# One diffusion-transformer layer on one core: stores moved to ScalarE's queue, results of the output products added one group later

## The chip, the core and the metric

The kernel runs on one NeuronCore of a Trainium2 chip. The metric is the device time of one execution in microseconds. The core has a matrix engine (TensorE, "PE" in the profile; "PEld" is its loading of weights), a vector engine (VectorE, DVE), a scalar or activation engine (ScalarE, ACT), a general engine (GpSimd, POOL) and a synchronization engine (SyncE, SP). Each works off its own list of instructions in order; between engines they wait on semaphores. A DMA transfer is issued by an instruction in some engine's list, and runs afterwards on the DMA engines.

## The reference

The layer has 1024 latent tokens and 256 context tokens of width 1024, all in fp32. Cut to what matters:

```python
def swiglu(h, w_in, w_out):
    a, b = jnp.split(h @ w_in, 2, axis=-1)
    return (jax.nn.silu(a) * b) @ w_out

mod_lat = jax.nn.silu(c) @ w_mod + b_mod            # nine vectors ml[0..8]; mc[...] from c_ctx
x  = x  + 0.5 * ml[2] * swiglu(modulate(rms_norm(x,  g1), ml[0], ml[1]), ffn1_w_in, ffn1_w_out)
cx = cx + 0.5 * mc[2] * swiglu(modulate(rms_norm(cx, g1), mc[0], mc[1]), ffn1_w_in, ffn1_w_out)
hx = modulate(rms_norm(x, g2), ml[3], ml[4])        # the same for the context
bg, cg, vc, q, k, v, gates = split(hx @ w_in)
y_conv = bg * short_conv(cg * vc, conv_w)
o = attention(q, k, v)                              # 8 query heads, 2 key heads, QK norm, 2-D rotary
x = x + ml[5] * merge_branches(y_conv, o, gates, w_bc, w_ba, w_out)
x = x + 0.5 * ml[8] * swiglu(modulate(rms_norm(x, g3), ml[6], ml[7]), ffn2_w_in, ffn2_w_out)
return rms_norm(x, final_g)
```

The hidden width of both feed-forward blocks is 2816, 22 blocks of 128.

## The kernel before

**Precision.** Each fp32 operand is split into a high part (a cast, on ScalarE) and a low part (source minus high part, on VectorE). A product is three matmuls: high·high, high·low and low·high.

**The big products** go through the class `Winograd`, a scheme that computes a 2×2 block product with seven block products. For each pair `j` of weight columns, `first` computes products 1 and 2 (result `u`, `c`), `second` products 6, 7 and 4 (result `v`, `b`), and `third` products 5 and 3 (results `u`, `v`). One block product is twelve matmuls of 128×512. Its left operand comes from a weight load (`raw`, three buffers, loaded from SyncE's queue) or from a sum of two halves of one (`s1`, `s2`, `s3`, built on GpSimd), and is split into a tile `wl` or `wh` (four buffers each); `prefetch(4)` keeps four such tiles ready. Its right operand, `r1` to `r7`, is made once from the normalized tokens. `r1` and `r2` come from the first half of the tokens (`norm0`), `r5` and `r6` from both halves, and the "late" ones `r7`, `r4`, `r3` at the end of `norm1`.

Since products 1 and 2 need only the first half, `start` runs them for the first nine pairs (`AH2`, `AH3`) of the mixer's and of the second feed-forward block's product, while `norm1` is worked off step by step between them. All but the first two results `uc` are stored in DRAM (`put_aside`, tile `ucd`) and fetched again (`fetch`). What remains of `norm1` after that is kept as `self.late` and run in `second`. `norm1` is a generator with nine yields: the first for the row scales, the second for their broadcast, four for the columns, three for the late operands.

**The output products** of the two feed-forward blocks go through `row_products`. It takes the seven products in the order 2, 1, 4, 6, 5, 7, 3; each runs over groups of two blocks of the hidden rows, and has four banks of PSUM. Products 1, 6 and 7 add up in the same four banks (`chain`). After a product, its banks are added, with the gate as a factor, into the token tiles `x` (a table `to` says which), and a callback `after` starts what depends on it. `sums`, the additions on the hidden rows, are issued in a block in which `strict[0]` is true.

**The order of the work.** The program is handed to `TileContext(schedule_with_timeline_sim=True)`, which moves instructions within their engine's list. While `strict[0]` is true, each instruction issued through the wrapper `Engine` (its `issue` is line 88, so that nearly every row of the profile says L88) is pinned: it keeps its place in program order relative to other pinned ones.

**Modulation.** `later_mod` is a generator that computes one half of one of the nine vectors: eight loads of `w_mod` rows (`rawm`), each with a multiply-add into `macc` on VectorE and a yield; then `WAIT` yields; the split of the sum (`acch` on ScalarE, `accl` on VectorE); six yields; then two matmuls, a copy, four small DMAs and an add. It is worked off in portions: `run(steps, n)` in the loop over `j` of the first feed-forward block, `run(late_steps, n)` in the mixer (5 + 4 + 4 per `i`) and in the second feed-forward block (3 per `j`).

**Stores.** Results that go to DRAM on the way are stored by `put_aside` (`ucd`, 22 stores), `spill` (the hidden rows, `hd`, 88), `gate` (`gcd`, `gad`) and the mixer's loop (`yd`), 48 together. All of these are issued by SyncE, whose queue also issues the loads of weights, of `rawm` and of the fetched tiles.

Of the kernel before, what the change touches and what calls it, by code (L numbers as in the profile page):

```python
# [41 lines left out]
STEPS = (0, 4, 4, 4, 5, 5, 5, 5, 5, 5, 5, 2, 12)  # L42
WAIT = 4
AH1, HALVES, WH = 12, 8, (4, 5, 6, 7, 12, 13, 14, 15, 20, 21, 22, 23)
# [5 lines left out]
def tile_dit_layer(  # L50
# [211 lines left out]
    def later_mod(m, halves=(0, 1), streams=None):  # L262
# [3 lines left out]
        for half in halves:  # L266
# [15 lines left out]
            for acc in accs:  # L282
                ah, al = ttile("acch", dt=F32R), ttile("accl", dt=F32R)
                split(acc, ah, al)
                parts.append((ah, al))
            for _ in range(6):
                yield
# [178 lines left out]
    class Winograd:  # L466
# [194 lines left out]
        def start(self, norm):  # L661

            for i in range(self.n_ahead):
                t = wpool.tile([P, 2, 512], F32, tag="wh", name=uniq("uc"), bufs=W_BUFS)
                u, c = t[:, 0], t[:, 1]
                act.copy(out=u, in_=self.product(1))
                run(norm, 2 if i == 0 else 1)
                dve.tensor_add(out=c, in0=u, in1=self.product(2))
                if i < RESIDENT:
                    self.started.append((u, c))  # L670
                else:
                    self.put_aside(t)
            run(norm, 9 - self.n_ahead)
            self.prefetch(4)
            self.late = norm

        def put_aside(self, t):
            ucd = dram.tile([P, 2, 512], F32, name=uniq("ucd"))
            sp.dma_start(out=ucd[:], in_=t[:])
            self.started.append(ucd)  # L680
# [62 lines left out]
        def second(self, u):  # L743

            v, b = ttile("v"), ttile("b")
            dve.tensor_add(out=u, in0=u, in1=self.product(6))
            run(self.late, 4)
            dve.tensor_add(out=v, in0=u, in1=self.product(7))
            if self.side:
                self.side(0, self.left())  # L750
            dve.tensor_sub(out=b, in0=v, in1=self.product(4))
            run(self.late)
            return v, b

        def third(self, u, v):
# [39 lines left out]
    def row_products(w, rows, add, after=lambda i, k: None, halves=False):  # L795
# [112 lines left out]
        }  # L908
        chain = None
        for i in (2, 1, 4, 6, 5, 7) + (() if halves else (3,)):  # L910
# [3 lines left out]
            for g, (k, m) in enumerate(groups):  # L914
# [4 lines left out]
                strict[0] = True  # L919
                sums(i, g)  # L920
                strict[0] = False
                after(i, k)
            for o, ch in to[i]:
                for d in range(4):
                    add(o + d, ch, ps[d])
            after(i, rows.n)
        if halves:
            kept = []
            ps = [ps_s(256) for _ in range(4)]
            for k, m in groups:  # L930
                for lr in operands(3, k, m):
                    step(3, ps, len(kept), *lr, n=256)
                    kept.append(lr)
                after(8, k)
            for d in range(4):
# [243 lines left out]
    def spill(a, b, j, ch):  # L1179
        act.activation(out=a, in_=a, func=AF.Silu)  # L1180
        dve.tensor_mul(out=a, in0=a, in1=b)
        sp.dma_start(out=hd[j, :, ch[1] : ch[1] + 512], in_=a)

# [46 lines left out]
    for j in range(NH):  # L1230
        half1.side = side(j) if j >= SIDE_FROM else None
        if j > SIDE_FROM and j % 2:
            raws = context_rows(j)
        u, c = half1.next_first()
        v, b = half1.second(u)
        spill(c, b, j, C0)
        spill(*half1.third(u, v), j, C1)
        run(steps, STEPS[min(j, len(STEPS) - 1)])
        if j == SIDE_FROM - 1:
# [55 lines left out]
    def after1(i, k):  # L1295
# [16 lines left out]
        if k == NH // 2:  # L1312
# [4 lines left out]
            elif i == 3:  # L1317
                done(range(4), C1)
        if i == 3 and k in (0, 4):
            run(norms2, 1)  # L1320
# [19 lines left out]
    def gate(dst, j, ch, g):  # L1340
        act.activation(out=g, in_=g, func=AF.Sigmoid)
        sp.dma_start(out=dst[j, :, ch[1] : ch[1] + 512], in_=g)

    for i in range(KD):
# [6 lines left out]
        for ch, bg, gc in mixed():  # L1351
# [12 lines left out]
            dve.tensor_mul(out=y, in0=y, in1=bg)  # L1364
            sp.dma_start(out=yd[i, :, o : o + 512], in_=y)
        if i % 2:
# [475 lines left out]
    for j in range(NH):  # L1842
        if j > 1:
            run(late_steps, 3)
        u, c = fast.next_first()
        v, b = fast.second(u)
        spill(c, b, j, C0)
        spill(*fast.third(u, v), j, C1)
    run(late_steps)
    gate3 = half_gate("gate3", 8)  # L1850
# [75 lines left out]
```

## Time and profile before

| | |
|---|---|
| median of 3 runs | 2688.97 us (2684.92 to 2689.53) |
| the profiled execution itself | 2688.7 us |
| its span on the core | 2686.9 us |
| granted clock, mean | 0.993 |
| matmul instructions | 13593 |

The span goes from the first to the last instruction of the profiled execution; the rest of its time lies around that. A row of a timeline has the start in us, the duration, the engine, the line, the operation with its tiles (out<-in), and the number of such operations in a row; in brackets stands how long the engine stood idle before it, and whose work ended that. A row of waits has the waiting engine and tile, the engine and tile waited for, the total in us, the number of times and the longest. A group has its line, engine, operation and number, the busy time, the mean in ns, and the idle time before. SPq is SyncE's queue; a row of it is the issue of a DMA, not its transfer. Tile names in the profile and in the order are without their buffer numbers.

Along the span, the first feed-forward block's first product takes the time up to about 640 us, its output product up to 887, the mixer's product follows up to about 1300, then attention and merge, and the second feed-forward block ends the span.

### The profile page before, as it was taken

To read this page: it belongs to the slowest core of one execution; us is meant where nothing else is said; L and a number is where in the kernel's file an instruction comes from. 1 tells how busy PE (TensorE), PEld (TensorE's weight loads), DVE (VectorE), ACT (ScalarE), POOL (GpSimd) and SP (SyncE) were. 2 spreads that over 40 slices of the span, in tenths; PEclk is the share of its full clock that TensorE was granted. 3 is DMA by queue.
4 is the path that set the end of the run, shared out by engine and by line. 5 is a ranking of instruction groups with operands and counts; after the bars stand their busy time and mean duration, and the time that the engine had idled before them with its cause. 6 is when DMAs were issued, how large, how long until landed. Compare 5 with 4: busy or idle time off the path is not lost.

```text
span 2686.9 us, 37399 instructions
## 1 busy us (share of the span) xinstructions
PE 2643.4 (98%) x13593; PEld 2236.0 (83%) x13593; DVE 2007.1 (75%) x3356; ACT 1166.1 (43%) x2317; POOL 521.3 (19%) x409
## 2 busy tenths in 40 slices
PE   8999999999999999999999999999999999999998
PEld 5788898888788877888999888877888888888888
DVE  5888888786887889877488666775458875667875
ACT  6633543333454632333244666674236333334543
POOL 1244012121110044232033111000001533230200
PEclk9999999999999999999999999999999999999998
DMA  7655653346973445433213211002524543228731
GB/s 267 236 180 166 223 184 124 109 130 240 293 169 102 149 137 165 134 114 116 97 48 103 95 62 49 24 25 78 167 85 146 184 145 99 83 90 305 165 83 63
DMA packets 369920, 364.84 MB, mean 136 GB/s; under 512 B 27830, under 2 KB 261448, under 8 KB 369736
## 3 DMA queue, kind: packets, MB, share of 16 engines
q1 hardware_dynamic: 360712, 345.17, 39.0%
q0 software_dynamic: 9024, 17.30, 4.0%
q8 instruction: 106, 1.74, 0.3%
q14 instruction: 78, 0.64, 0.1%
HBM read 296.30 MB, written 66.06 MB: 135 GB/s over the span
## 4 chain that ended last, share of the span: by engine, by line
PE 88%; DVE 6%; DMA 2%; ACT 2%; issue 1%; SPq 1%; POOL 0%; DVEq 0%; ACTq 0%; POOLq 0%
PE ps L88 73%; PE po L88 7%; PE pt L88 7%; DMA rawm<-in_w_mod_dram 1%; DVE macc L88 1%; DVE wl L88 1%; SPq L88 1%; DVE xb L88 0%; DVE r L88 0%; ACT r L88 0%; DMA raw<-in_ffn_w_in_dram 0%; DMA xtok<-in_ctx_dram 0%; DVE ol L88 0%; DVE x L88 0%; DVE pts L88 0%
## 5 line engine op out<-in xcount | busy, mean ns | idle before, releaser
L88 PE MATMUL ps<-r,wl 128*128 128x512 f32 x5232 | 1213.4, 392 | 11.6 <-ACT wl L88 6.8
L88 PEld LDWEIGHTS ps<-r,wl 128*128 128x128 f32 x5232 | 983.9, 189 | 220.0 <-ACT wl L88 9.0
L88 ACT CAST wl<-s 128x512 fp32r<-128x512 f32 x256 | 158.0, 620 | 338.3 <-PE ps L88 266.6
L88 POOL TENSOR_TENSOR s<-raw 128x512 f32<-128x512 f32 x64 | 92.4, 1444 | 993.8 <-PE ps L88 346.6
L88 ACT CAST wl<-raw 128x512 fp32r<-128x512 f32 x286 | 176.4, 619 | 250.0 <-PE ps L88 160.6
L88 DVE TENSOR_TENSOR wl<-raw,wl 128x512 fp32r<-128x512 f32 x284 | 202.6, 717 | 68.3 <-ACT wl L88 64.7
L88 DVE TENSOR_TENSOR wl<-s,wl 128x512 fp32r<-128x512 f32 x256 | 231.8, 906 | 12.3 <-ACT wl L88 10.7
L88 POOL TENSOR_TENSOR s<-raw,s 128x512 f32<-128x512 f32 x64 | 99.8, 1560 | 363.9 <-DVE wl L88 354.4
L88 DVE SCALAR_TENSOR_TENSOR macc<-rawm,silu_c,macc 128x512 f32<-128x512 f32 x168 | 137.9, 837 | 9.5 <-DMA rawm<-in_w_mod_dram 9.1
L88 PE MATMUL ps<-wh,r 128*128 128x256 f32 x768 | 141.6, 285 | 0.0
L88 DVE TENSOR_TENSOR pts<-pt,pts 128x512 fp32r<-128x512 f32 x160 | 108.8, 687 | 39.4 <-ACT pts L88 38.4
L88 DVE TENSOR_TENSOR u<-u,ps 128x512 f32<-128x512 f32 x168 | 114.2, 680 | 28.5 <-PE ps L88 28.4
L88 DVE TENSOR_REDUCE m<-ps 128x1 f32<-128x512 f32 (+1 forms) x192 | 110.9, 596 | 31.0 <-PE ps L88 30.3
L88 ACT CAST pts<-pt 128x512 fp32r<-128x512 f32 x160 | 93.2, 593 | 88.7 <-PE pt L88 86.8
L88 ACT CAST rh<-hid 128x512 fp32r<-128x512 f32 x132 | 81.6, 621 | 112.2 <-PE ps L88 96.2
L88 PE MATMUL ps<-rh,wl 128*128 128x512 f32 x360 | 122.0, 389 | 0.0
L88 PEld LDWEIGHTS ps<-wh,r 128*128 128x128 f32 x768 | 120.6, 192 | 0.0
L88 ACT CAST wh<-raw 128x512 fp32r<-128x512 f32 (+1 forms) x88 | 69.3, 795 | 103.0 <-PE ps L88 79.5
L88 PE MATMUL po<-pts,vh 128*128 128x512 f32 x256 | 110.5, 437 | 1.5 <-ACT pts L88 1.5
L88 DVE TENSOR_TENSOR rl<-hid,rh 128x512 fp32r<-128x512 f32 x132 | 90.1, 686 | 26.5 <-ACT rh L88 13.5
L88 PE MATMUL ps<-wl,r 128*128 128x256 f32 x384 | 108.8, 283 | 0.0
L88 PE MATMUL ps<-kl,qs 128*128 128x512 f32 x384 | 105.3, 397 | 0.0
(298 smaller groups left out, 5068.1 us busy)
## 6 DMA issues: line engine op xcount, KB each, us to landing
raw<-in_ffn_w_in_dram SPq DMA_DIRECT2D x125, 512.0 KB
raw<-in_ffn_w_out_dram SPq DMA_DIRECT2D x72, 512.0 KB
rawm<-in_w_mod_dram SPq DMA_DIRECT2D x128, 256.0 KB
raw<-in_w_in_dram SPq DMA_DIRECT2D x61, 512.0 KB
hid<-hd SPq DMA_DIRECT2D x40, 512.0 KB
ws<-in_ffn_w_out_dram POOLq DMA_DIRECT2D x30, 512.0 KB, 6.6
ucd<-uc SPq DMA_DIRECT2D x22, 512.0 KB
hd<-c SPq DMA_DIRECT2D x38, 256.0 KB
```

Of the source, the lines that this page charges most:

```text
L88: inst = getattr(self.engine, name)(*args, **kw)
```

## The change

Seven edits:

1. `WAIT` goes from 4 to 2, and the second wait in `later_mod` from six yields to three.
2. In `start`, the step of `norm` is run only for `i < 9`.
3. The stores `ucd`, `hd`, `gcd`, `gad` and `yd` are issued by ScalarE (`act.dma_start`) and not by SyncE.
4. In `second`, the runs of `self.late` go through `late_operands`, which pins what they issue.
5. In `row_products`, a product's results are not added right behind it but kept in `results`, and added behind the first group of the next product, in the pinned block of `sums`; `after(i, rows.n)` moves with them. Only the last product's adds stay at its end.
6. The portions of `steps` and `late_steps` in the two feed-forward blocks are split in three and run between `next_first`, `second` and `third`, not once per `j`.
7. During product 3 of the first output product, the two steps of `norms2` run at `k` 2 and 6 and not 0 and 4.

```diff
-WAIT = 4
+WAIT = 2
...
-            for _ in range(6):
+            for _ in range(3):
                 yield
...
-                run(norm, 2 if i == 0 else 1)
+                run(norm, 2 if i == 0 else 1 if i < 9 else 0)
...
-            sp.dma_start(out=ucd[:], in_=t[:])
+            act.dma_start(out=ucd[:], in_=t[:])
...
-            run(self.late, 4)
+            self.late_operands(4)
...
-            run(self.late)
+            self.late_operands()
             return v, b
+
+        def late_operands(self, n=None):
+            strict[0] = True
+            run(self.late, n)
+            strict[0] = False
...
-        chain = None
+        chain, results = None, []
+
+        def add_results():
+            while results:
+                i, ps = results.pop()
+                for o, ch in to[i]:
+                    for d in range(4):
+                        add(o + d, ch, ps[d])
+                after(i, rows.n)
+
...
                 strict[0] = True
                 sums(i, g)
+                add_results()
                 strict[0] = False
                 after(i, k)
-            for o, ch in to[i]:
-                for d in range(4):
-                    add(o + d, ch, ps[d])
-            after(i, rows.n)
+            results.append((i, ps))
+        if not halves:
+            add_results()
...
-        sp.dma_start(out=hd[j, :, ch[1] : ch[1] + 512], in_=a)
+        act.dma_start(out=hd[j, :, ch[1] : ch[1] + 512], in_=a)
...
+        n_steps = STEPS[min(j, len(STEPS) - 1)]
         u, c = half1.next_first()
+        run(steps, n_steps // 3)
         v, b = half1.second(u)
         spill(c, b, j, C0)
+        run(steps, n_steps // 3)
         spill(*half1.third(u, v), j, C1)
-        run(steps, STEPS[min(j, len(STEPS) - 1)])
+        run(steps, n_steps - n_steps // 3 * 2)
...
-        if i == 3 and k in (0, 4):
+        if i == 3 and k in (2, 6):
             run(norms2, 1)
...
-        sp.dma_start(out=dst[j, :, ch[1] : ch[1] + 512], in_=g)
+        act.dma_start(out=dst[j, :, ch[1] : ch[1] + 512], in_=g)
...
-            sp.dma_start(out=yd[i, :, o : o + 512], in_=y)
+            act.dma_start(out=yd[i, :, o : o + 512], in_=y)
...
-        if j > 1:
-            run(late_steps, 3)
+        n_steps = j > 1
         u, c = fast.next_first()
+        run(late_steps, n_steps)
         v, b = fast.second(u)
         spill(c, b, j, C0)
+        run(late_steps, n_steps)
         spill(*fast.third(u, v), j, C1)
+        run(late_steps, n_steps)
```

What this makes of the order is shown at three places. The first is SyncE's list before, towards the end of the first block's loop over pairs (`u` and `c` are fetched tiles, `raw` weight loads; `in_ffn_w_out_dram` is the block's second weight):

```order
L88 DMA u_2308<-ucd_1048 128x512
L88 DMA hd<-u_2054 128x512
L88 DMA c_2309<-ucd_1048 128x512
L88 DMA hd<-c_2164 128x512
L88 DMA raw_2482<-in_ffn_w_in_dram 128x8x128
L88 DMA raw_2550<-in_ffn_w_out_dram 128x1024
L88 DMA raw_2552<-in_ffn_w_out_dram 128x1024
```

The same place of SyncE's list in the changed kernel:

```order
L88 DMA u_2090<-ucd_942 128x512
L88 DMA c_2091<-ucd_942 128x512
L88 DMA raw_2270<-in_ffn_w_in_dram 128x8x128
L88 DMA raw_2578<-in_ffn_w_out_dram 128x1024
L88 DMA raw_2580<-in_ffn_w_out_dram 128x1024
L88 DMA raw_2272<-in_ffn_w_in_dram 128x8x128
```

The stores to `hd` have left the list, and the two loads of `ffn_w_out` stand earlier against the loads of `ffn_w_in` and the fetches.

The second is VectorE's list before, where product 2 of the first output product ends and product 1 begins (`x` are token tiles, `ps` the banks of product 2, `wl` the low part of product 1's first weight, `hid` sums on the hidden rows):

```order
L88 TENSOR_TENSOR hid_6558<-hid_6559,hid_6558 128x1024
L88 SCALAR_TENSOR_TENSOR x_1159_6794<-ps_6582,gate_l,x_1159_6794 128x512
L88 SCALAR_TENSOR_TENSOR x_1160_6796<-ps_6583,gate_l,x_1160_6796 128x512
L88 SCALAR_TENSOR_TENSOR x_1161_6798<-ps_6584,gate_l,x_1161_6798 128x512
L88 SCALAR_TENSOR_TENSOR x_1162_6800<-ps_6585,gate_l,x_1162_6800 128x512
L88 TENSOR_TENSOR hid_6560<-hid_6560,hid_6558 128x1024
L88 TENSOR_TENSOR rl_7015<-hid_6566,rh_7014 128x512
L88 TENSOR_TENSOR wl_6920<-raw_6918,wl_6920 128x512
```

The same place of VectorE's list in the changed kernel:

```order
L88 TENSOR_TENSOR hid_6558<-hid_6559,hid_6558 128x1024
L88 TENSOR_TENSOR rl_7015<-hid_6566,rh_7014 128x512
L88 SCALAR_TENSOR_TENSOR x_1159_6794<-ps_6582,gate_l,x_1159_6794 128x512
L88 TENSOR_TENSOR wl_6916<-raw_6914,wl_6916 128x512
L88 SCALAR_TENSOR_TENSOR x_1160_6796<-ps_6583,gate_l,x_1160_6796 128x512
L88 SCALAR_TENSOR_TENSOR x_1161_6798<-ps_6584,gate_l,x_1161_6798 128x512
L88 SCALAR_TENSOR_TENSOR x_1162_6800<-ps_6585,gate_l,x_1162_6800 128x512
```

The split of `wl` stands behind one of the four adds, and no longer behind all of them and a sum.

The third is ScalarE's list of the changed kernel, where the mixer's nine started pairs end (`r` are the late operands from `t` and `h`, `uc` a started result, `wl` from `s` the first weight of the next product):

```order
L88 CAST r_1536_8869<-t_1498_8699 128x512
L88 COPY uc_8955<-ps_8959 128x512
L88 CAST r_1537_8872<-t_1511_8756 128x512
L88 CAST r_1545_8914<-h_1472_8586 128x512
L88 CAST r_1546_8917<-h_1484_8641 128x512
L88 CAST r_1547_8920<-h_1497_8698 128x512
L88 CAST r_1548_8923<-h_1510_8755 128x512
L88 CAST wl_8936<-s_1552_8931 128x512
```

These rows stand word for word in ScalarE's list before, too: here nothing has moved.

More of the change, by code (lines that the diff above doesn't have):

```diff
@@ L933, in row_products @@
                     kept.append(lr)
+                add_results()
                 after(8, k)
```

## The prediction

> **What bounds the kernel now.** I read the page's busy shares first, then windows of undisturbed stretches, then the waits of TensorE and the timelines around the longest of them.
>
> ```profile
> span 2686.9 us, 37399 instructions
> PE 2643.4 (98%) x13593; PEld 2236.0 (83%) x13593; DVE 2007.1 (75%) x3356; ACT 1166.1 (43%) x2317; POOL 521.3 (19%) x409
> ```
> ```profile
> 936.00:956.00 20.00, 14.95 (x55) 11.76 (x54) 14.99 (x24) 12.17 (x26) 7.39 (x5) 0.83 0.41 135
> 1054.00:1070.00 16.00, 13.43 (x46) 10.17 (x45) 15.59 (x21) 4.33 (x8) 8.47 (x7) 0.79 0.30 95
> 1100.00:1200.00 100.00, 100.00 (x443) 82.57 (x442) 79.38 (x114) 33.40 (x57) 33.53 (x23) 1.00 0.40 124
> ```
>
> TensorE is busy 98% of the span. A saturated stretch holds 443 matmuls of 512 columns in 100 us (third windows row; the columns are the window, its length, busy time and count of PE, PEld, DVE, ACT and POOL, the granted clock, the DMA share and GB/s). So a matmul is 0.226 us and a product of twelve is 2.71 us. The first two rows are gaps: 55 matmuls in 20 us where 88.6 fit, so 33.6 × 0.226 = 7.6 us lost; 46 in 16 us where 70.9 fit, so 5.6 us lost. Part of both losses is the granted clock, 0.83 and 0.79 there against 1.00.
>
> The change touches no matmul, so it can act only on time in which TensorE stands. The waits of TensorE (total us, times, longest) that lie near what is edited:
>
> ```profile
> PE ps L88 <- ACT wl L88: 8.0, 4, 5.1
> PE ps L88 <- DVE wl L88: 3.0, 3, 1.8
> PE pt L88 <- DVE wl L88: 1.7, 1, 1.7
> PE ps L88 <- ACT uc L88: 1.3, 1, 1.3
> PE pt L88 <- DMA xtok<-in_ctx_dram: 0.6, 1, 0.6
> ```
>
> The five rows sum to 14.6 us; with the slow clock behind the two long gaps and some small waits in the tail, that is what the change could win. The terms below go by place.
>
> **Stores off SyncE.** 158 stores (22 `ucd`, 88 `hd`, 48 of gates and `y`) leave SyncE's queue. Where one of them waits there, the loads behind it wait too. One such place shows on TensorE, at 258–288 us:
>
> ```profile
> 257.75 0.42 SPq L88 DMA_DIRECT2D c<-ucd  x1
> 265.29 0.32 SPq L88 DMA_DIRECT2D hd<-c  x1
> 266.44 0.38 SPq L88 DMA_DIRECT2D raw<-in_ffn_w_in_dram  x1
> 266.88 1.26 SPq L88 DMA_DIRECT2D raw<-in_ffn_w_out_dram  x2
> ```
> ```profile
> 272.91 1.14 ACT L88 CAST wo<-raw 128x512 fp32r<-128x512 f32 x2 [5.06 <-DMA raw<-in_ffn_w_out_dram]
> ```
> ```profile
> 277.32 0.39 PE L88 MATMUL ps<-h1ch,wl 128*128 128x256 f32 x1 [1.13 <-ACT wl L88]
> 280.58 0.50 PE L88 MATMUL ps<-h1ch,wl 128*128 128x256 f32 x2 [0.18 <-DVE wl L88]
> 287.43 0.51 PE L88 MATMUL ps<-h1ch,wl 128*128 128x256 f32 x2 [1.80 <-DVE wl L88]
> ```
>
> SyncE issued nothing from 258.17 (257.75 + 0.42) to 265.29, over 7 us, because its next instruction was the store of `c`. The weight loads came right behind it; the ones of `ffn_w_out` landed at 272.9, ScalarE's cast had waited 5.06 us for them, and TensorE stood 1.13 + 0.18 + 1.80 = 3.1 us. In the changed order (first pair of order pieces above) the store is gone and the two loads stand behind an earlier load. A load issued at 266.9 and landed at 272.9 takes 6.0 us; issued 7 us sooner it is in time, since the cast waited only 5.06. Bounds: nothing (the buffers of `raw` are still full, or the bus still busy) to −3.1; the 7 us is over the 5.06, so I take **−3.1**.
>
> At the start, four `ucd` stores stand ahead of the context's token loads:
>
> ```profile
> 76.92 2.20 SPq L88 DMA_DIRECT2D ucd<-uc  x3
> 80.42 1.40 SPq L88 DMA_DIRECT2D ucd<-uc  x1
> 87.91 1.61 SPq L88 DMA_DIRECT2D xtok<-in_ctx_dram  x2
> ```
>
> They held SyncE 3.6 us. TensorE's waits for these tokens and for `uc` are 0.6 and 1.3 us. Bounds 0 and −1.9; SyncE was also waiting for other things between 82 and 88, so I take half, **−1.0**.
>
> What the 158 issues cost on ScalarE isn't in the trace, which has no DMA issued there. The bounds are rows of other queues:
>
> ```profile
> L88 SPq DMA_DIRECT2D hd<-c x38: 319/327/477, 177.3 to 2441.3; - x38
> 690.65 1.36 POOL L88 DMA_DIRECT2D ws<-in_ffn_w_out_dram  x1 [55.27 <-PE ps L88]
> ```
> ```profile
> ACT wl L88 <- PE ps L88: 440.1, 256, 5.7
> L88 DVE TENSOR_TENSOR wl<-s,wl 128x512 fp32r<-128x512 f32 x256 | 231.8, 906 | 12.3 <-ACT wl L88 10.7
> ```
>
> At SyncE's 0.33 us it is 158 × 0.33 = 52 us of ScalarE's time, at GpSimd's 1.36 it is 215; I take 0.33, a queue that like ScalarE's does little else while it issues. ScalarE is busy 43%, and in 256 waits it stood 440 us only because TensorE hadn't freed a weight buffer. What hides the issues is the lead of the weights: three ready products ahead, 3 × 2.71 = 8.1 us, less a cast (0.62, the duration of the row on `acch` below) and a VectorE split (0.9) = 6.6 us. Each store stands behind the silu and the multiply whose result it writes, so a wait there is of the order of one product, 2.7 us. Sum **0**; if the cover is gone, what remains of that wait is exposed in full (the slower rival).
>
> **Results one group later.** At the change of product in the output product (VectorE's rows above), four adds stood ahead of the split of the next product's first weight:
>
> ```profile
> 701.81 2.72 DVE L88 SCALAR_TENSOR_TENSOR x<-ps,gate_l,x 128x512 f32<-128x512 f32 x4
> 706.18 0.68 DVE L88 TENSOR_TENSOR wl<-raw,wl 128x512 fp32r<-128x512 f32 x1
> ```
> ```profile
> 703.11 0.50 PE L88 MATMUL pt<-rh,wl 128*128 128x512 f32 x1 [1.39 <-ACT wl L88]
> 706.92 0.73 PE L88 MATMUL pt<-rh,wl 128*128 128x512 f32 x2 [1.67 <-DVE wl L88]
> ```
>
> The second wait, 1.67 us, ends with the split at 706.18 + 0.68. In the changed order one add (2.72 / 4 = 0.68) is ahead of the split, not four: it comes some 2 us sooner and the wait goes, **−1.7**. The first, 1.39 us, waits for the cast of a load, which no edit moves: it stays. At other product changes TensorE waits nowhere, so there the edit is worth 0; the four banks stay full for one group more, which costs nothing because the products take four banks of tag s and the four of `chain` in turn, so that the next one wants others; if it wanted the same, it would be up to two blocks, 5.4 us.
>
> In the tail of the last output product eight adds stood before the last splits:
>
> ```profile
> 2628.03 1.10 PE L88 MATMUL ps<-kept,kept 128*128 128x256 f32 x7 [0.35 <-DVE x L88]
> 2629.63 2.53 PE L88 MATMUL ps<-kept,kept 128*128 128x256 f32 x19 [0.27 <-DVE kept L88]
> ```
>
> 0.35 + 0.27: **−0.6**, or 0 if the adds only pile up later.
>
> **Late operands pinned.** `norm1` yields nine times and `start` already runs it 2 + 8 = 10 times with nine products ahead, so `late` is empty when `second` comes: the new pin holds nothing, and the count `if i < 9` changes nothing either. The order of ScalarE shows the twelve casts of late operands ahead of `wl<-s` both times. So the longest gap stays:
>
> ```profile
> 936.17 3.74 ACT L88 CAST r<-t 128x512 fp32r<-128x512 f32 x7
> 942.89 1.14 ACT L88 CAST wl<-s 128x512 fp32r<-128x512 f32 x2
> ```
> ```profile
> 943.57 1.65 PE L88 MATMUL ps<-r,wl 128*128 128x512 f32 x3 [5.05 <-ACT wl L88]
> ```
>
> **Steps and WAIT.** The same loads and adds come in smaller portions and, with 2 and 3 idle steps for 4 and 6, sooner after each other. One gap hangs on a step of `later_mod`, at 1050–1060:
>
> ```profile
> 1049.98 0.62 ACT L88 CAST acch<-macc 128x512 fp32r<-128x512 f32 x1 [3.80 <-DMA raw<-in_w_in_dram]
> 1057.01 0.62 ACT L88 CAST wl<-s 128x512 fp32r<-128x512 f32 x1 [6.41 <-POOL s L88]
> ```
> ```profile
> 1053.04 1.47 POOL L88 TENSOR_TENSOR s<-raw 128x512 f32<-128x512 f32 x1 [10.38 <-DVE accl L88]
> 1055.60 1.37 POOL L88 TENSOR_TENSOR s<-s,raw 128x512 f32<-128x512 f32 x1 [1.09 <-DMA yd<-y]
> ```
>
> The cast `acch` held ScalarE, its partner `accl` held the tile that GpSimd's sum needed, the next sum waited for a store of `y`, and TensorE lost the 5.6 us above. The changed program has the same chain of tiles there, with the store now on ScalarE: I leave it, **0**, with −5.6 and +7.6 (the other gap) as bounds.
>
> The norm that moves by two groups of product 3 has its last matmuls, a broadcast, 39 matmuls ahead of the mixer's first product:
>
> ```profile
> 878.12 9.11 PE L88 MATMUL ps<-wh,wl 128*128 128x512 f32 x39
> ```
>
> In the changed order there are 40 between the two: **0**.
>
> **Sum.** The profiled execution took 2688.7 us (span 2686.9), the median of the runs is 2688.97: the same within 0.3 us. 2688.7 − 3.1 − 1.0 − 1.7 − 0.6 = **2682.3 us**. About 0.2%, 5.4 us, is what a measurement can tell from no change, so the bounds of "same" about the median are 2683.6 and 2694.4: the forecast lies 1.3 us beyond the lower.
>
> **Rivals.**
>
> *The stores bring nothing.* Place 258–288 keeps its wait but for the issue of the store itself, 0.32 us, because `raw` buffers or the bus hold the loads. For it: SyncE waits most for VectorE's `wl`, which frees those buffers; against it: the 7 us of silence on the queue. 2688.7 − 0.3 − 1.7 − 0.6 = 2686.1, no change. The Trainium skill, page "DMA: Bandwidth & Descriptors", section "Issuing engines are not separate DMA queues", speaks for this rival: transfers started by different engines share the same 16 DMA engines, and several issuers save only the sequencer's time, "usually small relative to the DMA itself". By that rule the time is 2686.1; the row at 265.29 speaks against it, since there the queue was held by a wait and not by the issue.
>
> ```profile
> SPq L88 <- DVE wl L88: 619.7, 152, 52.3
> ```
>
> *The modulation stalls ScalarE more often (slower).* With fewer idle steps, the cast `acch` comes sooner behind the last load of its sum. In the changed order of the mixer two of five `acch` casts stand close behind their last loads and ahead of `yd` stores, `u` copies and weight casts. Each such cast is a stall like the one at 1050 as soon as it waits longer than the lead of 6.6 us. Price per stall between 5.6 and 7.6 us, mean 6.6: 2682.3 + 13.2 = 2695.5. For it: ScalarE's queue now also carries the stores, so every wait holds more. Against it: three of four `acch` casts in the mixer stalled nothing.
>
> *The pin works* (the forecast takes that edit as empty): the gap at 938 goes, 2682.3 − 7.6 = 2674.7. Against it stands the order.
>
> *The gap at 1050 goes*, because the modulation's steps fall elsewhere: 2682.3 − 5.6 = 2676.7. For it: its loads are now spread; against it: the chain of tiles is the same.
>
> **How the numbers follow.** Forecast 0.40, of which 0.28 lie below 2683.6, since the start's term alone, halved once more, would not bring it back, and 0.12 above; stores bring nothing 0.20, all same; gap at 1050 goes 0.15 and pin works 0.07, faster; more modulation stalls 0.18, of which 0.14 slower and 0.04 same. Faster 0.28 + 0.15 + 0.07 = 0.50; same 0.12 + 0.20 + 0.04 = 0.36; slower 0.14. The range goes from 2674, the pin's case, to 2696, the modulation's: what is left out is half of each and mixtures of them. The forecast's own range is 2679 (start and a little slow clock in full) to 2686 (start and store at nothing).
>
> **What would show it.** Right: no wait of SyncE ahead of the `ffn_w_out` loads, no wait for ACT or DVE `wl` near 277–288, only one wait near 703, ScalarE's DMA issues near 0.33 us. Wrong: new rows of ACT `wl` among TensorE's waits in the mixer, with an `acch` or a store ahead of them; or the 5.05 gap gone; or a time outside 2674–2696.

## The result, and the profile after

The changed kernel took 2693.59 us (median of 9 runs, 2690.41 to 2697.46), the kernel before 2685.34 us (9 runs, 2682.46 to 2689.53). The ratio is 1.0029, with a 95% interval of 1.0020 to 1.0039: about 8 us slower, where the prediction's sum had it 6.4 us faster (2682.3 against 2688.7). The profiled executions lie 4.2 us apart (2692.86 against 2688.7), because the one of before lies near the upper end of its nine runs; what follows reads places, not the difference of two spans.

The page of the changed kernel: as many matmuls, as busy, on a longer span.

```profile
span 2690.8 us, 37348 instructions
PE 2642.7 (98%) x13593; PEld 2232.8 (83%) x13593; DVE 2007.8 (75%) x3356; ACT 1167.3 (43%) x2317; POOL 523.8 (19%) x409
```

TensorE's waits in the changed kernel (total us, times, longest):

```profile
PE ps L88 <- ACT wl L88: 9.8, 5, 5.0
PE ps L88 <- DVE wl L88: 5.1, 6, 1.6
PE ps L88 <- ACT u L88: 2.0, 1, 2.0
PE ps L88 <- DVE u L88: 1.2, 1, 1.2
PE pt L88 <- DVE wl L88: 0.6, 2, 0.3
PE ps L88 <- DVE x L88: 0.3, 1, 0.3
PE ps L88 <- DVE kept L88: 0.3, 1, 0.3
```

The wait of 5.0 in the first row is the gap at 938 us (here at 948.8), untouched. `pt` for DVE `wl` fell from 1.7 to 0.6 and `pt` for ACT `wl` is gone: the place at 703 us was relieved. The last two rows, the tail, are as before. New are the waits for `u` and more waits for `wl`, and one of 0.98 us at 677 us for `cacc`, which takes back part of the relief at 703. Windows show where; first the kernel before, then the changed one.

```profile
236.00:276.00 40.00, 40.00 (x178) 32.53 (x176) 34.30 (x60) 14.49 (x29) 13.48 (x9) 1.00 0.54 172
1084.00:1104.00 20.00, 20.00 (x90) 16.53 (x89) 18.86 (x28) 8.05 (x14) 6.23 (x5) 1.00 0.51 170
```
```profile
236.00:276.00 40.00, 34.20 (x137) 25.70 (x136) 37.23 (x58) 12.12 (x23) 12.99 (x10) 0.96 0.48 152
1084.00:1104.00 20.00, 17.96 (x79) 14.54 (x78) 19.00 (x28) 6.09 (x11) 6.65 (x4) 1.00 0.47 153
```

From 236 to 276 us, the last pairs of the first feed-forward block's loop, TensorE was busy all the time before; now it stands 5.8 us. At 1084 to 1104, in the mixer, it stands 2.0 us. The first of these places, engine by engine, in the timelines of the changed kernel: SyncE, GpSimd, VectorE, ScalarE, TensorE.

```profile
249.65 11.29 SPq L88 DMA_DIRECT2D rawm<-in_w_mod_dram  x4
261.03 0.38 SPq L88 DMA_DIRECT2D raw<-in_ffn_w_in_dram  x1
```
```profile
250.90 1.41 POOL L88 TENSOR_TENSOR s<-raw 128x512 f32<-128x512 f32 x1 [10.48 <-DVE u L88]
```
```profile
252.30 2.45 DVE L88 SCALAR_TENSOR_TENSOR macc<-rawm,silu_c,macc 128x512 f32<-128x512 f32 x2 [0.55 <-DMA rawm<-in_w_mod_dram]
254.84 0.69 DVE L88 TENSOR_TENSOR b<-v,ps 128x512 f32<-128x512 f32 x1
255.57 0.87 DVE L88 TENSOR_TENSOR c<-c,b 128x512 f32<-128x512 f32 x1
```
```profile
254.24 0.62 ACT L88 CAST wl<-s 128x512 fp32r<-128x512 f32 x1 [2.49 <-POOL s L88]
256.47 0.36 ACTq L88 DMA_DIRECT2D hd<-c  x1
256.93 0.62 ACT L88 CAST wl<-s 128x512 fp32r<-128x512 f32 x1 [2.08 <-DVE c L88]
```
```profile
254.91 0.73 PE L88 MATMUL ps<-r,wl 128*128 128x512 f32 x2 [0.81 <-ACT wl L88]
257.60 4.59 PE L88 MATMUL ps<-r,wl 128*128 128x512 f32 x13 [1.96 <-ACT wl L88]
```

Read from the bottom: TensorE waited for a cast at 256.93; that cast stood behind a store which waited for `c`; `c` and `b` stood on VectorE behind two multiply-adds of the modulation, which began by waiting for their row; the sum that the other cast needed had waited 10.5 us on GpSimd; and SyncE took 11.3 us for four loads of modulation rows with a weight load behind them. One such issue takes 0.33 us; most of the rest were waits, the two longest for `c` and for the store of `c` to land:

```profile
SPq L88 <- DVE c L88: 4.1, 1, 4.1
SPq L88 <- DMA hd<-c: 3.3, 1, 3.3
```

Before, no modulation row was loaded between 212 and 268 us. The second place, in the mixer:

```profile
1092.53 0.62 ACT L88 CAST acch<-macc 128x512 fp32r<-128x512 f32 x1 [5.16 <-DVE macc L88]
1093.49 0.58 ACT L88 COPY u<-ps 128x512 f32<-128x512 f32 x1 [0.35 <-DMA raw<-in_w_in_dram]
```
```profile
1094.13 4.19 PE L88 MATMUL ps<-r,wl 128*128 128x512 f32 x17 [2.04 <-ACT u L88]
```

ScalarE's cast `acch` waited 5.16 us for the sum, behind it stood the copy that empties a bank, and TensorE waited for the bank.

These rows hold two suspects, the stores on ScalarE (edit 3) and the steps of the modulation (edits 1 and 6). The experiments part them.

### The profile page after: what moved, and what is told of

It reads as the page before. It is cut to its first block, busy times and chain, and to the rows that moved or that the text cites. A ratio compares the mean times of both kernels' runs of the same rounds, so it can differ in the third digit from the quotient of the medians.

```text
span 2690.8 us, 37348 instructions
## 1 busy us (share of the span) xinstructions
PE 2642.7 (98%) x13593; PEld 2232.8 (83%) x13593; DVE 2007.8 (75%) x3356; ACT 1167.3 (43%) x2317; POOL 523.8 (19%) x409
## 4 chain that ended last, share of the span: by engine, by line
PE 81%; DVE 4%; DMA 2%; ACT 1%; issue 1%; SPq 0%; POOL 0%; DVEq 0%; ACTq 0%; POOLq 0%
PE ps L88 67%; PE po L88 7%; PE pt L88 7%; DVE wl L88 1%; DMA rawm<-in_w_mod_dram 1%; DVE macc L88 0%; DMA x<-xd 0%; DVE ol L88 0%; DVE x L88 0%; DVE r L88 0%; SPq L88 0%; ACT pts L88 0%; DVE nt L88 0%; ACT r L88 0%; DVE pts L88 0%
## 5 line engine op out<-in xcount | busy, mean ns | idle before, releaser
L88 DVE TENSOR_TENSOR wl<-s,wl 128x512 fp32r<-128x512 f32 x256 | 219.3, 858 | 13.6 <-ACT wl L88 11.2
```

Of the source, the lines that this page charges most:

```text
L88: inst = getattr(self.engine, name)(*args, **kw)
```

## The experiments

To compare places, I took from each profile TensorE's lost time: over all its matmuls, the time from its start to the next one's start, less the median of that for the same shape, added up by stretch. It holds waits and slow clock, and it comes from one profiled execution of each kernel. So the column 900–1080 moves by itself: at the gap of 1057 us TensorE's waits are 2.6 us before and 2.9 in the changed kernel (there at 1063), but the lost time is 6.0 and 3.6 us, because the granted clock over the 20 us from 3 us ahead of the gap was 0.83 and 1.00. Ratios are to the kernel before on the same chip, from five rounds, with their 95% intervals; the medians of different rows are not to be compared, since the kernel before itself took 2686.6 to 2687.6 us there.

| kernel | 240–300 | 300–400 | 400–640 | 640–720 | 900–1080 | 1080–1130 | median us | ratio (interval) |
|---|---|---|---|---|---|---|---|---|
| before | 4.5 | 0.0 | 0.7 | 4.4 | 14.1 | -0.1 | | |
| changed | 8.7 | 1.5 | 0.5 | 3.1 | 11.1 | 2.4 | 2693.59 | 1.0029 (1.0020–1.0039) |
| stores_alone | 2.2 | 0.0 | 0.5 | 4.4 | 14.5 | -0.1 | 2685.42 | 0.9994 (0.9985–1.0002) |
| stores_back | 9.3 | 3.6 | 2.5 | 3.3 | 10.9 | 2.2 | 2696.54 | 1.0042 (1.0029–1.0056) |
| results_alone | 4.9 | 0.0 | 1.0 | 4.5 | 12.1 | -0.1 | 2688.71 | 1.0003 (0.9995–1.0012) |
| steps_alone | 8.8 | 2.1 | 4.3 | 3.3 | 9.1 | 2.2 | 2694.75 | 1.0031 (1.0020–1.0042) |
| wait_alone | 9.2 | 2.5 | 7.8 | 3.1 | 11.1 | 1.9 | 2697.76 | 1.0039 (1.0027–1.0052) |
| thirds_alone | 3.1 | 0.0 | 0.5 | 4.3 | 11.1 | -0.1 | 2683.17 | 0.9989 (0.9979–0.9999) |
| wait_back | 3.9 | 0.0 | 0.5 | 6.5 | 14.1 | 0.0 | 2688.89 | 1.0004 (0.9996–1.0013) |
| thirds_back | 10.9 | 0.8 | 6.8 | 2.6 | 13.8 | 1.1 | 2699.00 | 1.0039 (1.0026–1.0053) |
| phase_shift | 10.2 | 2.6 | 0.5 | 3.2 | 10.0 | 0.0 | 2692.80 | 1.0025 (1.0016–1.0035) |
| wait_phase | 2.3 | 1.1 | 12.3 | 3.2 | 12.9 | 0.3 | 2697.92 | 1.0043 (1.0030–1.0056) |
| wait_noadds | 4.9 | 0.0 | 0.5 | 3.2 | 8.2 | 0.6 | 2683.76 | 0.9991 (0.9982–1.0000) |
| wait_noloads | 4.8 | 6.0 | 0.5 | 3.2 | 10.1 | 3.1 | 2691.76 | 1.0021 (1.0011–1.0030) |
| wait_ring13 | 5.9 | 5.7 | 4.6 | 5.1 | 10.3 | 2.8 | 2701.73 | 1.0050 (1.0038–1.0063) |
| ring13 | 2.5 | 0.7 | 0.7 | 7.8 | 9.3 | 0.1 | 2690.57 | 1.0013 (1.0004–1.0022) |
| thirds_stores | 3.5 | 0.1 | 0.5 | 7.2 | 13.9 | -0.1 | 2687.31 | 1.0004 (0.9995–1.0013) |
| late_real | 3.2 | 0.2 | 0.6 | 4.4 | 9.0 | 0.0 | 2690.01 | 1.0014 (1.0005–1.0023) |
| idle_7_3 | 1.7 | 0.2 | 0.8 | 4.6 | 8.4 | 0.0 | 2683.61 | 0.9990 (0.9981–0.9999) |
| idle_2_8 | 5.5 | 0.0 | 5.4 | 6.1 | 14.1 | -0.1 | 2691.49 | 1.0021 (1.0012–1.0029) |

### Which edit

**stores_alone**: before, with the four kinds of stores on ScalarE.

```diff
-            sp.dma_start(out=ucd[:], in_=t[:])
+            act.dma_start(out=ucd[:], in_=t[:])
...
-        sp.dma_start(out=hd[j, :, ch[1] : ch[1] + 512], in_=a)
+        act.dma_start(out=hd[j, :, ch[1] : ch[1] + 512], in_=a)
```

(and the same for `gate` and `yd`.)

> The kernel before with edit 3 alone (158 stores issued by ScalarE). Theory Q, that the stores now hold ScalarE's queue ahead of weight casts (in the changed kernel's profile the store of c at 256.5 us waits for VectorE and the cast behind it ends TensorE's wait of 1.96): slower than before by 4 to 10 us. Rival S, that the steps of the modulation do the harm (four rawm loads hold SyncE for 11.3 us at 249.7): this kernel has no such change and is up to 3 us faster than before, since the place at 258 to 288 us is relieved.

It is not slower: 0.9994, an interval that holds 1. Theory Q falls. The three waits at 275 to 290 us became one (first row below); but SyncE's waits from 255 to 268 us (second block) show that the loads hardly came sooner. In place of 7.0 us for the store's `c`, SyncE now waits 8.5 us for GpSimd to free the buffer of `raw`, and issued the `ffn_w_out` loads at 265.98 us, after 266.88 before.

```profile
285.39 0.50 PE L88 MATMUL ps<-h1ch,wl 128*128 128x256 f32 x2 [1.80 <-DVE wl L88]
```
```profile
SPq L88 <- POOL s L88: 8.5, 1, 8.5
```

The price of an issue on ScalarE, which the trace of before could not show, is in the tile view (minimum, median and maximum in ns):

```profile
L88 ACTq DMA_DIRECT2D hd<-c x38: 326/326/362, 178.2 to 2439.9; - x38
```

It is 0.33 us, SyncE's price.

**stores_back**: the changed kernel with the diff above reversed.

> The changed kernel with the 158 stores back on SyncE. Theory Q: the loss of 8 us is gone and the gain of the results' later adds stays, so 0 to 3 us faster than before. Rival S: still slower than before by 4 us or more, with rawm loads ahead of weight loads near 250 us.

Still slower by 0.42%: rival S. The stores were not the loss; with the steps as they are now, ScalarE is no worse a place for them (the two intervals overlap).

**results_alone**: before, with `add_results` in `row_products`, and `norms2` at `k` 2 and 6.

> The kernel before with edits 5 and 7 alone (results added one group later, the norm's steps at groups 2 and 6). Both theories: faster by 1.5 to 3 us, since the two waits of 1.39 and 1.67 us at the change of product near 703 us became 0.28 and 0.32 in the changed kernel; nothing else moves by over 1 us. A third possibility, that the pinned adds cost elsewhere: slower by 4 us or more.

The place at 703 us is not relieved. VectorE's list and TensorE's waits there:

```profile
703.62 2.72 DVE L88 SCALAR_TENSOR_TENSOR x<-ps,gate_l,x 128x512 f32<-128x512 f32 x4
707.99 0.68 DVE L88 TENSOR_TENSOR wl<-raw,wl 128x512 fp32r<-128x512 f32 x1
```
```profile
705.17 0.50 PE L88 MATMUL pt<-rh,wl 128*128 128x512 f32 x1 [1.65 <-ACT wl L88]
708.73 0.74 PE L88 MATMUL pt<-rh,wl 128*128 128x512 f32 x2 [1.42 <-DVE wl L88]
```

The four adds still stand ahead of the split, the waits add up to 3.07 us as before (3.06), and the time is 1.0003 where both theories had said 1.5 to 3 us faster. So neither the order nor the gain that I ascribed to this edit is its own.

**steps_alone**: before with edits 1 and 6.

> The kernel before with edits 1 and 6 alone (shorter idle steps, portions in thirds). Theory Q: within 3 us of before. Rival S: slower by 4 to 10 us, with a stall near 250 us behind rawm loads and one more in the mixer near 1090 us behind an acch.

1.0031, as slow as the whole change, with the losses at 240–300 and 1080–1130, and with the relief at 640–720. Rival S holds. The next four part it.

**wait_alone** and **wait_back**: edit 1 alone, and the changed kernel without it.

```diff
-WAIT = 4
+WAIT = 2
...
-            for _ in range(6):
+            for _ in range(3):
                 yield
```

> The kernel before with edit 1 alone (idle steps 2 and 3 for 4 and 6), the portions as before. Theory W: the loss comes from the shorter generator, which brings eight rawm loads every 14 steps and not every 19, so that its loads fall into other pairs and hold SyncE ahead of weight loads: slower by 4 to 9 us, with the stalls near 250 and 1095 us. Rival T, that it is the portions in thirds: within 3 us of before, the stalls near 250 us absent.

> The changed kernel with the idle steps at 4 and 6 again. Theory W: the loss is gone, 0 to 5 us faster than before. Rival T: still slower by 4 us or more.

**thirds_alone** and **thirds_back**: edit 6 alone, and the changed kernel without it.

> The kernel before with edit 6 alone (portions in thirds between the products), the idle steps as before. Theory W: within 3 us of before. Rival T: slower by 4 to 9 us, with the stalls near 250 us.

> The changed kernel with the portions in one piece again, the idle steps at 2 and 3. Theory W: still slower than before by 4 us or more. Rival T: the loss is gone, 0 to 5 us faster than before.

All four answer alike. With the short idle steps it is 0.39% slower (both times); without them 0.04% over before, within the error, or 0.11% faster. Edit 1 is the loss, edit 6 is a small gain. The sum of single effects (-0.06, +0.03, -0.11, +0.39) is 0.25%, near the 0.29 measured. wait_alone also has the relief at 640–720 (3.1). It goes with the modulation being done sooner, which edit 1 does: the last small DMA of a column is issued at 572 us and not at 668. phase_shift below, whose idle steps are those of before, has it too (3.2, last one at 647.5), while thirds_alone and wait_back (664 and 666) do not. Why the place hangs on it is not shown.

### Why shorter idle steps cost time

With 4 + 6 idle steps, `later_mod` takes 8 + 4 + 6 + 1 = 19 steps for each half vector, with 2 + 3 it takes 14. Two halves come ahead of the third vector, so its loads begin ten steps, two pairs of five, earlier in the loop: in wait_alone from 241 us, and not from 268. The context's norm is worked off by the same generator, between those halves and the third vector, and moves with the loads: its first product `nt` is made at 227 us and not at 254.

**phase_shift**: before, idle steps as they were, ten more steps in the middle pairs.

```diff
-STEPS = (0, 4, 4, 4, 5, 5, 5, 5, 5, 5, 5, 2, 12)
+STEPS = (0, 4, 4, 4, 7, 7, 7, 7, 7, 5, 5, 2, 12)
```

> The kernel before with its idle steps at 4 and 6, but ten more steps of the modulation in pairs 4 to 8 of the first feed-forward block (the table STEPS has 7 for 5 there), so that the loads of the third vector begin before the last pairs end, as with the short idle steps. Theory P, that the loss comes from where these loads and their multiply-adds fall, the last two pairs, where the context's norm and the first pieces of the second weight are made too: TensorE loses 3 to 6 us between 240 and 300 us more than before, and the time is 2 to 7 us longer. Rival R, that it comes from the denser loads as such: within 2 us of before.

The loss at 240–300 came with it, 10.2 us against 4.5, and 0.25% in time: theory P. TensorE's waits there are like those of the changed kernel:

```profile
253.85 0.73 PE L88 MATMUL ps<-r,wl 128*128 128x512 f32 x2 [1.62 <-ACT wl L88]
255.53 17.23 PE L88 MATMUL ps<-r,wl 128*128 128x512 f32 x60 [0.95 <-ACT wl L88]
```

The edit moves the context's norm too (first `nt` at 228 us). So it shows that the place of the generator's steps costs this time, not which of them does.

**wait_phase**: the short idle steps, with a table that keeps the loads out of the last pairs.

```diff
+WAIT = 2
...
+STEPS = (0, 4, 4, 4, 4, 4, 3, 3, 3, 4, 4, 2, 12)
```

> The kernel before with the short idle steps, but with a STEPS table (4, 4, 3, 3, 3, 4, 4 for pairs 4 to 10) that keeps the third vector's loads out of the last pairs. Theory P: the loss between 240 and 300 us is that of before, 4 to 5 us and not 9; what was lost later, 400 to 640 us and near 1100, stays, so the time is 2 to 7 us longer than before and 4 to 6 us shorter than with the short idle steps alone. Rival R: as slow as the short idle steps alone, about 11 us over before.

The place itself obeyed: 2.3 us at 240–300, fewer than before. But 400–640 rose from 7.8 to 12.3 us, and the time is no shorter: about 11 us over before, the number of rival R, though not for its reason. By the count of steps the new table moves the loads of all later vectors too, which theory P's number had left out.

**wait_noadds** and **wait_noloads**: what in the modulation holds the others, its multiply-adds or its loads? (Both on top of wait_alone.)

```diff
-    dve.scalar_tensor_tensor(out=acc, in0=raw, scalar=s, in1=acc, ...)
+    dve.scalar_tensor_tensor(out=acc[:, :8], in0=raw[:, :8], scalar=s, in1=acc[:, :8], ...)
```

> The kernel before with the short idle steps, its loads of modulation rows all made, but seven of each eight multiply-adds cut to 8 of 512 columns, so the modulation isn't computed in full (left out: most of VectorE's work on it, 0.74 us each). Theory V, that VectorE, full in the last pairs, is what is late: the losses of TensorE between 240 and 300 us fall to 2 us or less, and those of 400 to 640 us too. Rival L, that SyncE's queue or the DMA engines are: they stay at 9 and 8 us.

> The kernel before with the short idle steps and all multiply-adds, but with one load of modulation rows of each eight, the adds reading the sum itself instead, so the modulation isn't the reference's. Theory V: the losses of TensorE between 240 and 300 us stay within 3 us of 9, unless it was the wait for the row that held VectorE. Rival L: they fall to 3 us or less, those of 400 to 640 us too, and no wait of POOL for raw loads is over 2 us there.

Neither alone is the answer. Each halves the loss at 240–300 (4.9 and 4.8 of 9.2) and removes that of 400–640; without the loads 300–400 even rises to 6.0. In the whole time the adds weigh more: 0.9991 without most of them, 1.0021 without most loads. But these kernels do less work than the one before, and what it would take with as little was not measured. Nor is the place free in either: from 240 to 270 us, where before loses nothing and wait_alone 6.9 us, they still lose 3.9 and 4.4. The context's norm may hold this rest; it comes early in both (first `nt` at 225 and 224 us), and no run moves it without the loads. A chain in which any shortening helps would give such numbers; that is a reading, not shown. GpSimd's timeline of wait_alone points to a link that both share:

```profile
249.18 3.22 POOL L88 TENSOR_TENSOR s<-raw 128x512 f32<-128x512 f32 x1 [9.66 <-DVE macc L88]
...
267.86 1.85 POOL L88 TENSOR_TENSOR s<-raw 128x512 f32<-128x512 f32 x1 [10.58 <-DMA c<-ucd]
```

The sum `s` needs a tile of the ring of eleven small tiles, which rows, sums, splits, `u` and `c` share in the order in which they were asked for. **wait_ring13** and **ring13** widen it.

```diff
-A_BUFS = 38
+A_BUFS = 37
...
-    tpool = ctx.enter_context(tc.tile_pool(name="tpool", bufs=11))
+    tpool = ctx.enter_context(tc.tile_pool(name="tpool", bufs=13))
```

> The kernel before with the short idle steps and the ring of small tiles at 13 and not 11 (A_BUFS, the ring of large tiles, at 37 and not 38, which pays for it). Theory G, that GpSimd's sums come late because their tile of the ring is still held by the modulation: GpSimd's waits of 9.7 and 10.6 us near 249 and 268 us and most of the loss between 240 and 300 and between 400 and 640 us go, the time is within 4 us of before. Rival V, that VectorE's order is what holds: as slow as the short idle steps alone, 8 to 12 us over before.

> The kernel before with the ring of small tiles at 13 and A_BUFS at 37, the control to the run beside it. Theory G: 0 to 4 us faster than before, since the place near 1050 us, too, began with a sum that waited for a tile. Rival V: within 2 us of before. If the ring of large tiles was needed: slower.

GpSimd's waits did shrink,

```profile
243.62 1.46 POOL L88 TENSOR_TENSOR s<-raw 128x512 f32<-128x512 f32 x1 [5.20 <-DVE wl L88]
...
262.21 1.67 POOL L88 TENSOR_TENSOR s<-raw 128x512 f32<-128x512 f32 x1 [6.44 <-DMA raw<-in_ffn_w_in_dram]
```

and 240–640 lost 16.2 us instead of 19.5. But that is 3 us of the 14 that the short steps cost there (19.5 less the 5.2 of before), and the time was longer, not shorter. Theory G falls as the main cause. The large tile that paid for it was missed elsewhere: ring13 is 0.13% slower than before, and loses 7.8 us at 640–720 and 23.1 between 1130 and 1850 us, where before loses 4.4 and 16.7. So the whole time says little about the ring, and only the places count.

At 500 us wait_alone shows another form. VectorE, then TensorE:

```profile
505.48 0.16 DVE L88 TENSOR_TENSOR modc<-mcol,bcol 128x4 f32<-128x4 f32 x1 [1.79 <-DMA mcol<-mrow]
...
506.83 0.49 DVE L88 TENSOR_SCALAR macc<-rawm,silu_c 128x512 f32<-128x512 f32 x1 [0.79 <-DMA rawm<-in_w_mod_dram]
507.23 0.68 DVE L88 TENSOR_TENSOR c<-u,ps 128x512 f32<-128x512 f32 x1
```
```profile
507.97 4.29 PE L88 MATMUL ps<-r,wl 128*128 128x512 f32 x12 [1.88 <-DVE c L88]
```

The add that empties a bank stands on VectorE behind a 0.16 us add that waits for four small DMAs. That suggested that the second idle count (6 to 3), the distance between the split and that add, is what costs. **idle_7_3** and **idle_2_8** keep the sum of ten, so the loads stay where they were, and share it differently.

```diff
-WAIT = 4
+WAIT = 7
...
-            for _ in range(6):
+            for _ in range(3):
```

> The kernel before with seven idle steps before the split and three behind it, for four and six: the loads fall as before, the distance from the split to the columns is that of the changed kernel. Theory D, that this distance covers the chain of split, matmul, copy and small DMAs: VectorE stands on the adds of mcol with results behind them, TensorE loses 3 us or more between 400 and 640 us, the time is 3 to 8 us longer than before, and nothing is lost between 240 and 300 us beyond the 4.5 us of before. Rival P, that only where the loads fall counts: within 2.5 us of before.

> The kernel before with two idle steps before the split and eight behind it. Theory D: the distance is longer, no loss between 400 and 640 us, within 2.5 us of before. Rival, that the split too close behind the last load is what costs (ScalarE's cast acch waits, with weight casts behind it): 3 to 8 us longer, with TensorE's waits for ACT wl behind an acch.

The other way round: three steps behind the split and seven ahead are 0.10% faster than before, two ahead and eight behind 0.21% slower. Theory D falls: three steps behind the split do no harm if the loads stay in place, two ahead of it do, or the eight behind it, which keep the split's tiles longer: the two counts were not varied apart. idle_7_3 and thirds_alone are the two that compute the layer and beat both kernels, by 0.1% and 0.4%, the first figure just clear of its error. Most of the loss of idle_2_8 from 400 to 640 us, 4.9 of 5.4, is at 516 us. ScalarE, then TensorE:

```profile
517.65 1.34 ACT L88 CAST acch<-macc 128x512 fp32r<-128x512 f32 x2 [0.47 <-DVE macc L88]
518.89 0.58 ACT L88 COPY u<-ps 128x512 f32<-128x512 f32 x1
```
```profile
519.53 2.86 PE L88 MATMUL ps<-r,wl 128*128 128x512 f32 x6 [3.00 <-ACT u L88]
```

The copy that empties a bank stands behind two casts that wait for the last multiply-adds: the same form as at 1092 us in the changed kernel, and what the slower rival of the prediction described. But the form alone doesn't cost time. ScalarE of the kernel before:

```profile
560.78 1.34 ACT L88 CAST acch<-macc 128x512 fp32r<-128x512 f32 x2 [2.05 <-DVE macc L88]
562.03 0.58 ACT L88 COPY u<-ps 128x512 f32<-128x512 f32 x1
```

Here the casts waited longer, the copy stood right behind them as well, and TensorE went on: it ran two products from 560.49 to about 566 us without a stand. Why the copy at 518.89 was needed at once and this one was not, no run shows.

### Two more

**thirds_stores**: before with edits 3 and 6.

> The kernel before with edits 3 and 6 alone (stores on ScalarE, portions in thirds), the two that were not slower each by itself. If they add up (0.06% and 0.11%): 3 to 6 us faster than before. If they save the same wait, at 275 to 290 us: 1 to 3 us.

1.0004, within its error of no change, so the time of neither reading: the two small gains do not add up. Both had shortened 240–300 (2.2 and 3.1 us; together 3.5), and the change of product at 640–720 lost 7.2 and not 4.4.

**late_real**: the late operands really moved into `second`.

```diff
-                run(norm, 2 if i == 0 else 1)
+                run(norm, 2 if i == 0 else 1 if i < 5 else 0)
...
-            run(norm, 9 - self.n_ahead)
...
-            run(self.late, 4)
+            self.late_operands(1)
             dve.tensor_add(out=v, in0=u, in1=self.product(7))
+            self.late_operands(1)
```

> The kernel before with the late operands really moved: norm1 runs in start only to its four columns, and r7, r4 and r3 are made in second, pinned, one set after each of products 6, 7 and 4. If the gap at 938 us was the twelve casts ahead of the next weights: the wait of 5.05 goes, 4 to 8 us faster than before. If the casts are late anyway, because product 7 needs r7 2.7 us after product 6 begins: a new wait of 2 to 5 us there, and the time within 2 us of before.

Nearer the second reading. The gap of 5.05 us became two (first block), and the second feed-forward block, which lost 0.6 us between 1850 and 2100 before, now loses 3.1 (second block). The ratio, 0.14% or some 4 us over before, lies outside its 2 us, too. From 930 to 960 us the loss fell from 8.1 to 4.0; the rest of the fall in the column 900–1080 (9.0 against 14.1) is at the gap of 1057 us, where the clock differs. That the time did not follow is not explained by these places. The profiled execution was the fastest of its eleven.

```profile
941.85 5.73 PE L88 MATMUL ps<-r,wl 128*128 128x512 f32 x24 [1.29 <-DVE r L88]
949.70 10.53 PE L88 MATMUL ps<-r,wl 128*128 128x512 f32 x45 [2.11 <-DVE r L88]
```
```profile
2071.83 5.92 PE L88 MATMUL ps<-r,wl 128*128 128x512 f32 x24 [1.06 <-ACT r L88]
2079.13 6.23 PE L88 MATMUL ps<-r,wl 128*128 128x512 f32 x26 [1.38 <-DVE r L88]
```

## Why the prediction was wrong, point by point

**Steps and WAIT, 0.** This is the step that failed. I looked at one place that hangs on the modulation, 1050 us, found its chain of tiles unchanged, and wrote 0 for the edit with bounds of 5.6 and 7.6 us. That place did stay (waits of 2.6 us before, 2.9 after). I did not ask where the generator's loads, adds, casts and norm would fall once it was 14 steps long and not 19, though the table STEPS and the yields give that by counting. The edit alone costs 0.39%. Two parts of the cause are shown: steps of the generator that fall into the last pairs (phase_shift, 0.25%), and the idle count of 2 ahead of the split with 8 behind it, where a late cast stood ahead of a bank's copy (idle_2_8, 0.21%); in the changed kernel that form is the 2 us at 1092. How much VectorE, SyncE, the ring and the context's norm each hold in the first part stays open: the first three were shortened once each, and each time the loss shrank without going; the norm was never moved alone.

**The slower rival** had the right sign, part of the mechanism (an `acch` in ScalarE's queue) and nearly the time, 2695.5 against 2693.59. It named the mixer as the place, where one stall of 2.04 us came and not two of 6.6; the larger part was in the first feed-forward block. So the nearness of its time is luck: the gains for the stores and the start that it kept from the sum, 3.1 and 1.0 us, did not come, and its base was 2688.7 where the kernel before took 2685.34. I gave it 0.18.

**Stores, -3.1 and 0.** With the stores alone the waits at 275 to 290 us fell by 1.3 us, from 3.1 to 1.8 (the lost time there, with the slow clock, by 2.3), but not for the reason given: "issued 7 us sooner" was 0.9 us sooner, because the buffer of `raw` was the next thing that was late. That was the rival in which the stores bring nothing, and the whole is within its error of nothing, 0.9994. What issues cost on ScalarE was rightly taken as 0.33 us and hidden. The Trainium skill, "DMA: Bandwidth & Descriptors", section "Issuing engines are not separate DMA queues", says that several issuers save only the sequencer's time; the outcome agrees, no clear gain from 158 issues moved. The trace shows what stood behind it: the wait of 7.0 us taken from the queue was replaced by one of 8.5 us on the same queue.

**Start, -1.0.** Next to nothing: TensorE's lost time from 60 to 240 us is 4.9 before, 4.7 in the changed kernel and 4.1 with the stores alone. The tokens' wait is still 0.6. The wait for `uc` did go, from 1.32 to 0.18 us in the changed kernel, but a new one of 1.58 us for `wl` stands at 108 us; stores_alone has 0.72 and 0.97 there, and stores_back, with the stores on SyncE, 1.18, so the stores are not its only cause.

**Results one group later, -1.7 and -0.6.** The waits at 703 us fell from 3.06 to 0.60 in the changed kernel, the 1.39 that was to stay among them, but with the new wait at 677 us the stretch 640–720 gained only 1.3. And the relief is not edit 5's: edit 1 alone brings it, and with edit 5 alone the four adds stay where they were. I had read the order of the whole change and ascribed what moved to the edit that seemed to say so. The tail's 0.35 and 0.27 are still there.

**Late operands, 0.** Right: the pin held nothing, and the 5.05 us wait is 5.0. late_real shows that moving them in earnest changes the gap but brings its own.

**The norm's steps, 0.** Right: nothing is lost from 720 to 900 us before or after.

## What to carry to other kernels

Idle steps in a generator that is worked off between products are not waiting time to be saved: here they kept instructions with late inputs from standing ahead of others in a queue, and their sum set where every later step of the generator fell; count both before shortening them. A scheduler's order for a change of several edits attributes nothing to any of them: build each edit alone and read its order. And where a store is taken out of a queue, ask at once what that queue waits for next.

## What the runs showed that I had not expected

The issue of an `hd` store on ScalarE takes 0.326 us in the median, as on SyncE (0.327). A high busy share of VectorE was no sign of loss here: from 236 to 276 us it was busy for 38.36 of 40 us in wait_phase, where TensorE stood 0.3 us, and for 37.23 in the changed kernel, where TensorE stood 5.8.
